# Encoder layer on one core: constant decay rows loaded early, first chunk's products first, merge panels split on ScalarE and VectorE

## The chip, the cores and the metric

One Trainium2 chip, one of its cores. The metric is device time of one execution in microseconds (us). TensorE (PE) multiplies, VectorE (DVE), ScalarE (ACT) and GpSimd (POOL) work elementwise, SyncE (SP) issues the transfers (DMA). Each engine takes its instructions in the order of its own list and waits at the first whose inputs or buffers are not ready. SBUF is the on-chip memory, PSUM the accumulators that TensorE writes.

## The reference

One layer over two groups of tokens, a prompt of 512 and a sample of 1024, so 1536 tokens of width 1024:

```python
h = rmsnorm(x, norm_pre_mix)
q, k, v, z, xbc, dt_raw, gates = split(h @ w_in)
att = rmsnorm(diff_attention(q, k, v, lam, rel_bias), subln_w)
xs, B, C = split(silu(conv(xbc)))
y = ssd_scan(xs, dt_f, A_f, B, C) + flip(ssd_scan(flip(xs), flip(dt_b), A_b, flip(B), flip(C))) + d_skip * xs
y_ssm = rmsnorm(y * silu(z), ssm_norm_w)
merged = sigmoid(g0) * (att @ w_proj_attn) + sigmoid(g1) * (y_ssm @ w_proj_ssm)
x = x + rmsnorm(merged @ w_out, norm_post_mix)
h = rmsnorm(x, norm_pre_ffn)
x = x + rmsnorm((silu(h @ gate) * (h @ up)) @ w_down, norm_post_ffn)
```

The scan of the state-space branch (SSD) works in 12 chunks of 128 tokens. Inside a chunk it needs exp(a_cum[i] - a_cum[j]) below the diagonal, "the decays", for each of 16 heads and both directions.

## The kernel before, in words

All products are in fp32, as three products each: every operand is split into a high and a low part (hi = rounded value, lo = value - hi), and hi*hi, hi*lo and lo*hi are summed in PSUM. Lines L165 to L167 are these three. A weight panel is 1024 rows by 256 columns. `split_panel` (L145) loads it in two halves of 128x4x256 into `wraw` (pool `rp`, two buffers) and splits each with `split` (L133) into `whi` and `wlo` (pool `wp`, two buffers each). `split` has four forms: the default `act_dve` casts on ACT (L136) and subtracts on DVE (L137); `act_pool` subtracts on GpSimd; with `pool`, GpSimd does both (L142 the cast, L143 the subtraction).

The stages follow one another: normalisation of the tokens in three pieces of 512 (here called chunks c, `hT`, feature-major, transposed on TensorE, L203 to L205); projections for v, q, k, gates, dt and XBC, with attention over heads alongside; the SSD part with the projection for z alongside; the merge of both branches and the output projection; the feed-forward part. Intermediate tensors go through DRAM (`v_d`, `z_d`, `xs_d`, `ac_d`, `g_d` and so on). The order of each engine's list is set by a scheduler which simulates the program on its own timeline; the source only gives the data flow and the buffers.

**Start.** For c = 0, 1, 2: four token tiles are loaded, squared (ACT), scaled (L395, DVE) and transposed. After all three, the first two panels of v are loaded and split with `pool`, and their products are made per chunk.

**Decays.** One product with a matrix of 119 rows gives the decays. Its right operand `segr` (two tiles of 119 x 2048, one a direction) has 24 rows that depend on the steps (from `ac_d`, hi and lo, 12 each) and 95 constant rows (`c_neg`); the left operand `sl`, per chunk, has 24 selecting rows, 32 rows from `ad_d` and 63 constant ones (`c_sel`). `segr` is filled in four pieces of 1024 columns: three loads into `raw` (one buffer), one cast on DVE (L652). `c_neg` is loaded at that point, behind the stores of `ac_d`. The backward scan follows on the same SP queue: it loads `xg` (L690) and `bg`, scales xg on GpSimd (`xw`, L673), makes the state product `st_ps` on TensorE (L675) and the product `yo_ps` (L697).

**dt.** `wd` (the dt panel, 128x8x64) goes through `wraw` too; its product is L531. The XBC panels follow.

**Merge and output projection.** Their order in the source is out_proj(0), merge(1), norms(0), out_proj(1), merge(2), norms(1), operands of the feed-forward part, out_proj(2), norms(2). `merge` (L896) has four panels of w_proj_attn; per half panel the gate (`gt`, ACT L903) and the other branch (`pt`) are loaded, and the product is evacuated by DVE L907 (reads PSUM), L908, ACT L909 and DVE L910 into the split tiles `big`. `out_proj` has four panels of w_out and is evacuated by ACT. `norms` runs L1063 and L1064 (DVE), L1071 (DVE) and transposes for the feed-forward part (L1075). All 20 panels of the three out_proj and the two merge calls here are split with `pool`.

## Time and profile before

| | before |
|---|---|
| median of 3 runs | 3239.67 us (3237.82 to 3248.19) |
| profiled execution | 3245.1 us |
| its span | 3243.3 us |
| TensorE busy | 3049.5 us (94%) |
| DVE, ACT, POOL busy | 57%, 37%, 32% |
| mean granted TensorE clock | 0.974 |

The span runs from the first to the last recorded instruction. "Busy" is the time in which an engine executes, not that it does so at full rate: the granted clock tells at which share of its full clock TensorE was let run. An idle stretch of TensorE is listed with the instruction that it waited for and whatever ended the wait ("<-").

### The profile page before, as it was taken

To read this page: it belongs to the slowest core of one execution; us is meant where nothing else is said; L and a number is where in the kernel's file an instruction comes from. 1 tells how busy PE (TensorE), PEld (TensorE's weight loads), DVE (VectorE), ACT (ScalarE), POOL (GpSimd) and SP (SyncE) were. 2 spreads that over 40 slices of the span, in tenths; PEclk is the share of its full clock that TensorE was granted. 3 is DMA by queue.
4 is the path that set the end of the run, shared out by engine and by line. 5 is a ranking of instruction groups with operands and counts; after the bars stand their busy time and mean duration, and the time that the engine had idled before them with its cause. 6 is when DMAs were issued, how large, how long until landed. Compare 5 with 4: busy or idle time off the path is not lost.

```text
span 3243.3 us, 44646 instructions
## 1 busy us (share of the span) xinstructions
PE 3049.5 (94%) x16667; PEld 2677.0 (83%) x16667; DVE 1842.6 (57%) x2913; ACT 1209.3 (37%) x2255; POOL 1034.0 (32%) x796
## 2 busy tenths in 40 slices
PE   7999999999899999899999888878999899989998
PEld 7988887888787778687887777778999899978787
DVE  5114443455228994487788664776656766632444
ACT  4003333333113433466666523243333333322343
POOL 1003332000143442377567344433333433210100
PEclk9999999999999999999999998888999899999999
DMA  4623332223554454755555055544333333363354
GB/s 146 194 96 116 112 99 83 69 72 110 165 174 132 149 157 147 205 173 164 162 148 159 30 191 182 187 140 135 99 99 97 101 96 101 105 202 100 117 165 131
DMA packets 443325, 430.36 MB, mean 133 GB/s; under 512 B 25356, under 2 KB 360417, under 8 KB 442045
## 3 DMA queue, kind: packets, MB, share of 16 engines
q1 hardware_dynamic: 443109, 427.52, 42.8%
q8 instruction: 131, 2.15, 0.3%
q14 instruction: 85, 0.70, 0.1%
HBM read 315.37 MB, written 120.44 MB: 134 GB/s over the span
## 4 chain that ended last, share of the span: by engine, by line
PE 63%; DMA 12%; DVE 10%; issue 6%; POOL 4%; ACT 3%; SPq 1%; POOLq 0%; ACTq 0%; DVEq 0%
PE acc L165 9%; PE acc L167 9%; PE acc L166 9%; PE mm L165 5%; PE mm L167 5%; PE mm L166 5%; PE d L167 4%; PE d L166 3%; PE d L165 3%; DMA araw<-r_d 1%; DMA raw<-k_d 1%; DMA wraw<-in_w_gate_up_dram 1%; DMA gt<-g_d 1%; PE yd L772 1%; PE st_ps L675 1%
## 5 line engine op out<-in xcount | busy, mean ns | idle before, releaser
L165 PE MATMUL acc<-hT,whi 128*128 128x512 f32 x1056 | 420.9, 399 | 2.8 <-ACT st L435 2.8
L166 PE MATMUL acc<-hT,whi 128*128 128x512 f32 x1056 | 416.1, 394 | 0.0
L167 PE MATMUL acc<-hT,wlo 128*128 128x512 f32 x672 | 263.7, 392 | 0.0
L297 ACT ACTIVATE pt<-pt,nm 128x1024 f32<-128x1024 f32 (+1 forms) x192 | 193.3, 1008 | 125.5 <-DVE nm L294 115.3
L165 PEld LDWEIGHTS acc<-hT,whi 128*128 128x128 f32 x1056 | 198.5, 188 | 47.9 <-issue 5.5
L294 DVE CUSTOM_DVE_ANT_0 pt<-s,tb 128x1024 f32<-128x1024 f32 (+1 forms) x192 | 197.6, 1040 | 64.4 <-PE s L292 51.2
L166 PEld LDWEIGHTS acc<-hT,whi 128*128 128x128 f32 x1056 | 198.6, 188 | 42.2 <-issue 3.6
L165 PE MATMUL acc<-whi,hT 128*128 128x256 f32 x768 | 226.3, 295 | 0.1
L166 PE MATMUL acc<-wlo,hT 128*128 128x256 f32 x768 | 225.2, 293 | 0.0
L167 PE MATMUL acc<-whi,hT 128*128 128x256 f32 x768 | 224.2, 292 | 0.0
L167 PE MATMUL d<-dhi,fl 128*128 128x512 f32 x528 | 207.8, 394 | 8.3 <-DVE fl L137 8.3
L165 PE MATMUL d<-dhi,fh 128*128 128x512 f32 x528 | 207.7, 393 | 8.3 <-ACT fh L136 8.3
L166 PE MATMUL d<-dlo,fh 128*128 128x512 f32 x528 | 207.1, 392 | 0.0
L137 DVE TENSOR_TENSOR fl<-raw,fh 128x896 fp32r<-128x896 f32 (+1 forms) x72 | 85.9, 1195 | 200.4 <-ACT fh L136 200.4
L165 PE MATMUL mm<-op,wy 128*128 128x384 f32 x528 | 178.8, 339 | 10.3 <-ACT op L136 8.1
L167 PE MATMUL mm<-op,wy 128*128 128x384 f32 x528 | 178.7, 338 | 0.7 <-DVE wy L137 0.7
L166 PE MATMUL mm<-op,wy 128*128 128x384 f32 x528 | 178.3, 338 | 0.0
L303 POOL TENSOR_SCALAR pt<-pt,zs 128x512 f32<-128x512 f32 (+1 forms) x96 | 88.2, 919 | 255.4 <-DVE zs L301 213.5
L232 POOL TENSOR_TENSOR ql<-raw,qh 128x512 fp32r<-128x512 f32 x48 | 63.2, 1331 | 299.6 <-ACT qh L229 295.5
L165 PEld LDWEIGHTS acc<-whi,hT 128*128 128x128 f32 x768 | 148.6, 194 | 9.9 <-issue 8.5
L136 ACT CAST fh<-raw 128x896 fp32r<-128x896 f32 (+1 forms) x72 | 70.8, 983 | 227.7 <-PE d L166 212.7
L167 PE MATMUL acc<-hT,whi 128*128 128x512 f32 x384 | 155.5, 405 | 0.0
(358 smaller groups left out, 8612.6 us busy)
## 6 DMA issues: line engine op xcount, KB each, us to landing
wraw<-in_w_in_dram SPq DMA_DIRECT2D x60, 512.0 KB
wraw<-in_w_gate_up_dram SPq DMA_DIRECT2D x92, 256.0 KB
raw<-ff_d SPq DMA_DIRECT2D x48, 448.0 KB
wr<-in_w_gate_up_dram SPq DMA_DIRECT2D x80, 256.0 KB
ff_d<-c SPq DMA_DIRECT2D x88, 192.0 KB
g_d<-st SPq DMA_DIRECT2D x48, 256.0 KB
xg<-xs_d SPq DMA_DIRECT2D x48, 256.0 KB
gt<-g_d SPq DMA_DIRECT2D x48, 256.0 KB
```

Source lines behind the costliest of these rows:

```text
L136: S.copy(hi, raw)
L137: V.tensor_sub(lo, raw, f(hi))
L165: TE.matmul(ps, ah, bh, start=(i == 0), stop=False)
L166: TE.matmul(ps, ah, bl, start=False, stop=False)
L167: TE.matmul(ps, al, bh, start=False, stop=(i == n - 1))
L232: G.tensor_sub(q_l[:, s_], q_r[:, s_], f(q_h[:, s_]))
L294: V.tensor_tensor_reduce(out=pt[:], in0=sps[:], in1=tb[:, off:off + SL], scale=-1.0, scalar=3.0e38, op0=ALU.add, op1=ALU.min, accum_out=nm ...
L297: S.activation(out=pt, in_=pt, func=AF.Exp, bias=nm[:, m:m + 1], scale=-1.0, accum_out=(z0, zs[:, 0:1])[m])
L303: G.tensor_scalar(pm[1][:, cb], pm[1][:, cb], zs[:, 1:2], 0.0, op0=ALU.mult, op1=ALU.add)
L675: TE.matmul(ps, b_g, xw, start=True, stop=True)
L772: TE.matmul(yps[:, hs], ms[0][:, h, :], x_g[:, hs], start=True, stop=True)
```

## The change

- `segr` has 120 rows: 96 constant rows now come first, 24 step rows last, and `sl` accordingly (32 rows from `ad_d`, then 88 of `c_sel`: three loads instead of four). The constant rows are loaded in four loads of 96 x 1024 through `wraw` ahead of the dt panel, and cast on ACT. The step rows come late, in four loads of 12 x 2048 into two buffers of their own, and two ACT casts.
- v's first two panels are loaded directly behind chunk 0's tokens and split with a new form `pool_dve` (cast on GpSimd, subtraction on DVE). Chunk 0's products with the first panel follow chunk 0's transposes; those with the second panel come one chunk later.
- The panels of `merge` and `out_proj` are split with the default form, ACT and DVE.

```diff
-SEGK = 119
+SEGK = 120
...
     oh = (np.arange(32)[:, None] == bucket[None, :]).astype(np.float32)
     thr = np.arange(2, P, 2)
     sel = np.zeros((SEGK, 24, P), np.float32)
-    neg = np.zeros((2, SEGK - 24, NH, P), np.float32)
+    neg = np.zeros((2, 96, NH, P), np.float32)
     for r in range(24):
-        sel[r, [2 * (r % 12), 2 * (r % 12) + 1]] = 1.0
+        sel[96 + r, [2 * (r % 12), 2 * (r % 12) + 1]] = 1.0
     for r in range(32):
         neg[:, r, r % 16] = -1.0
-    sel[56:, 0::2] = (i[None, :] >= thr[:, None])[:, None, :]
-    sel[56:, 1::2] = (i[None, :] < thr[:, None])[:, None, :]
-    neg[0, 32:] = np.where(i[None, :] < thr[:, None], -1e30, 0.0)[:, None, :]
-    neg[1, 32:] = np.where(i[None, :] >= thr[:, None], -1e30, 0.0)[:, None, :]
-    return {"c_tri": c, "c_bucket": oh, "c_sel": sel, "c_neg": neg.reshape(2, SEGK - 24, NH * P)}
+    sel[32:95, 0::2] = (i[None, :] >= thr[:, None])[:, None, :]
+    sel[32:95, 1::2] = (i[None, :] < thr[:, None])[:, None, :]
+    neg[0, 32:95] = np.where(i[None, :] < thr[:, None], -1e30, 0.0)[:, None, :]
+    neg[1, 32:95] = np.where(i[None, :] >= thr[:, None], -1e30, 0.0)[:, None, :]
+    return {"c_tri": c, "c_bucket": oh, "c_sel": sel, "c_neg": neg.reshape(2, 96, NH * P)}
 
 
 @with_exitstack
...
     def split(hi, lo, raw, eng=None):
         if eng == "act_dve":
             S.copy(hi, raw)
+            V.tensor_sub(lo, raw, f(hi))
+        elif eng == "pool_dve":
+            G.tensor_scalar(hi, raw, 1.0, 0.0, op0=ALU.mult, op1=ALU.add)
             V.tensor_sub(lo, raw, f(hi))
         elif eng == "act_pool":
             S.copy(hi, raw)
...
         es = ExitStack()
         st0 = es.enter_context(tc.tile_pool(name="st0", bufs=4, reuse_waits="tile"))
         hT = []
+        def gemm_tm_pair(t, w):
+            ps = acc.tile([P, 2, 256], F32, tag="acc", name="acc")
+            for u in range(2):
+                gemm_tm(ps[:, u, :], w, hT[t // 4], slice((t + u) % 4 * P, ((t + u) % 4 + 1) * P))
+            return ps
+
+        def evac_v(p0, t, ps):
+            so = st0.tile([P, 2, 256], F32, tag="st0", name="st")
+            done = V.tensor_copy(so, ps)
+            store(out=v_d[t * P:(t + 2) * P, p0:p0 + 256].rearrange("(j p) n -> p j n", p=P), in_=so)
+            return done
+
         with tc.tile_pool(name="xa", bufs=2, reuse_waits="tile") as xa, tc.tile_pool(name="xa_ps", bufs=3, space=PSUM) as xps:
             natural_log_exp()
+            later = []
             for c in range(NCH):
                 dst = hp.tile([P, 2, KB, 512], F32R, tag="hT", name=f"hT{c}")
                 tiles = []
...
                     V.tensor_scalar(xt, xt, r[:, 0:1], 0.0, op0=ALU.mult, op1=ALU.add)
                 to_feature_major(xps, tiles, C_PRE, dst)
                 hT.append((dst[:, 0], dst[:, 1]))
+                for i in later:
+                    evac_v(i // 2 * 256, 4 * c - 4 + i % 2 * 2, gemm_tm_pair(4 * c - 4 + i % 2 * 2, first[i // 2]))
+                if c == 0:
+                    first = [split_panel(w_in[:, V0 + p0:V0 + p0 + 256], eng="pool_dve") for p0 in (0, 256)]
+                later = [2, 3]
+                for i in range(4 if c == NCH - 1 else 2):
+                    evac_v(i // 2 * 256, 4 * c + i % 2 * 2, gemm_tm_pair(4 * c + i % 2 * 2, first[i // 2]))
 
         def proj_fm(col0, ncol, evac, eng="act_dve", start=0):
             for p0 in range(start, ncol, 256):
...
                     so = st.tile([P, 512], F32, tag="st", name="st")
                     S.copy(so, ps)
                     store(out=g_d[r0:r0 + P, c * 512:(c + 1) * 512], in_=so)
-
-        def evac_v(p0, t, ps):
-            so = st0.tile([P, 2, 256], F32, tag="st0", name="st")
-            done = V.tensor_copy(so, ps)
-            store(out=v_d[t * P:(t + 2) * P, p0:p0 + 256].rearrange("(j p) n -> p j n", p=P), in_=so)
-            return done
-
-        first = [split_panel(w_in[:, V0 + p0:V0 + p0 + 256], eng="pool") for p0 in (0, 256)]
-        for c in range(NCH):
-            for i in range(4):
-                ps = acc.tile([P, 2, 256], F32, tag="acc", name="acc")
-                t = 4 * c + i % 2 * 2
-                for u in range(2):
-                    gemm_tm(ps[:, u, :], first[i // 2], hT[c], slice((t + u) % 4 * P, ((t + u) % 4 + 1) * P))
-                evac_v(i // 2 * 256, t, ps)
 
         with tc.tile_pool(name="pre2", bufs=1, reuse_waits="tile") as pre2, tc.tile_pool(name="pps2", bufs=2, space=PSUM) as pps2:
             lam = pre2.tile([P, 4, 64], F32, name="lam")
...
         dec = sp.tile([P, NT, 32], F32, name="dec")
         wst = sp.tile([P, NT, 32], F32, name="wst")
         segr = [sp.tile([SEGK, NH * P], F32R, name=f"segr{d_}") for d_ in range(2)]
+        for d_ in range(2):
+            for o in (0, 1024):
+                raw = staged(rp, [96, 1024], (None, a["c_neg"][d_][:, o:o + 1024]), tag="wraw")
+                S.copy(segr[d_][0:96, o:o + 1024], raw)
         dsk = sp.tile([P, NH], F32, name="dsk")
         load(out=dsk, in_=a["d_skip"].broadcast_to([P, NH]))
         wd = wp.tile([P, KB, 64], F32R, tag="whi", name="wd")
...
                 for i, t_ in enumerate((ah, al)):
                     store(out=d__[i].rearrange("(i c) h l -> (c h) i l", i=3), in_=f(t_[:, j]))
             for d_ in range(2):
-                for o in (0, 1024):
-                    os_ = slice(o, o + 1024)
-                    acv = [ac_d[s_].rearrange("(c d) h l -> c d (h l)", d=2)[:, d_, os_] for s_ in range(2)]
-                    raw = staged(dp, [SEGK, 1024], (slice(0, 12), acv[0]), (slice(12, 24), acv[1]),
-                                 (slice(24, SEGK), a["c_neg"][d_][:, os_]))
-                    V.tensor_copy(segr[d_][:, os_], raw)
+                acv = [ac_d[s_].rearrange("(c d) h l -> c d (h l)", d=2)[:, d_] for s_ in range(2)]
+                raw = staged(dp, [SEGK, NH * P], (slice(96, 108), acv[0]), (slice(108, 120), acv[1]), tag=f"raw{d_}")
+                S.copy(segr[d_][96:SEGK], raw[96:SEGK])
 
         dt_scope.close()
         sc = ph1.enter_context(tc.tile_pool(name="sc", bufs=2, reuse_waits="tile"))
...
             for c in range(lo_c, hi_c):
                 sl = sc.tile([SEGK, 2, P], F32R, tag="sl", name="sl")
                 acv = [ad_d[s_, 2 * c:2 * c + 2].rearrange("d h l -> h d l") for s_ in range(2)]
-                slr = staged(sc, [SEGK, 2, P], (slice(0, 24), a["c_sel"][0:24, 2 * c:2 * c + 2]),
-                             (slice(24, 40), acv[0]), (slice(40, 56), acv[1]),
-                             (slice(56, SEGK), a["c_sel"][56:SEGK, 2 * c:2 * c + 2]), tag="slr", bufs=1)
+                slr = staged(sc, [SEGK, 2, P], (slice(0, 16), acv[0]), (slice(16, 32), acv[1]),
+                             (slice(32, SEGK), a["c_sel"][32:SEGK, 2 * c:2 * c + 2]), tag="slr", bufs=1)
                 V.tensor_copy(sl, slr)
                 yz = wp.tile([P, 2, D], F32, tag="wlo", name="yz")
                 y, z = yz[:, 0], yz[:, 1]
...
             cs = slice(c * 512, (c + 1) * 512)
             hi, lo = big_pair()
             for p0 in range(0, D, 256):
-                w = split_panel(a["w_proj_attn"][0][:, p0:p0 + 256], eng="pool")
+                w = split_panel(a["w_proj_attn"][0][:, p0:p0 + 256])
                 for b in range(2):
                     r0 = p0 + b * P
                     kb = r0 // P
...
                 tiles = [mp.tile([P, D], F32, tag="mt", name="mt", bufs=4) for _ in range(4)]
                 sums = wk.tile([P, 4, 4], F32, tag="ms4", name="ms4")
                 for p0 in range(0, D, 256):
-                    w = split_panel(a["w_out"][0][:, p0:p0 + 256], eng="pool")
+                    w = split_panel(a["w_out"][0][:, p0:p0 + 256])
                     for j in range(4):
                         ps = mm_tile(256)
                         gemm_tm(ps, w, mT, slice(j * P, (j + 1) * P))
```

What the scheduler makes of it, at three places. The lists are those of one engine in order of issue; "x4" means four such instructions in a row.

SP at the start, up to chunk 1's tokens (`x_sample`); `wraw` is v's first panels. Before:

```order
L383 DMA prm<-in_subln_w_dram 1x128
L384 DMA prm<-in_conv_w_dram 60x128
L375 DMA xt<-in_x_sample_dram 128x1024 x4
L152 DMA wraw<-in_w_in_dram 128x4x256 x4
L375 DMA xt<-in_x_sample_dram 128x1024 x4
L152 DMA wraw<-in_w_in_dram 128x4x256 x2
```

With the change:

```order
L399 DMA prm<-in_subln_w_dram 1x128
L400 DMA prm<-in_conv_w_dram 60x128
L155 DMA wraw<-in_w_in_dram 128x4x256 x2
L391 DMA xt<-in_x_sample_dram 128x1024 x4
L155 DMA wraw<-in_w_in_dram 128x4x256 x4
L391 DMA xt<-in_x_sample_dram 128x1024 x4
```

The two halves of the first panel now go ahead of chunk 1's tokens, the second panel ahead of chunk 2's.

SP at the decays, behind the stores of `ac_d`, up to the first load of the backward scan (`xg`). Before:

```order
L131 DMA raw<-ac_d 12x1024 x4
L131 DMA raw<-in_c_neg_dram 95x1024
L645 DMA ad_d<-ah 128x3x128
L645 DMA ad_d<-al 128x3x128
L706 DMA z_d<-st 128x2x256
L131 DMA raw<-ac_d 12x1024 x2
L131 DMA raw<-in_c_neg_dram 95x1024
L706 DMA z_d<-st 128x2x256
L131 DMA raw<-ac_d 12x1024 x2
L131 DMA raw<-in_c_neg_dram 95x1024
L706 DMA z_d<-st 128x2x256
L690 DMA xg<-xs_d 128x512
```

With the change:

```order
L131 DMA raw_6447<-ac_d 12x2048
L131 DMA raw_6451<-ac_d 12x2048
L131 DMA raw_6447<-ac_d 12x2048
L131 DMA raw_6451<-ac_d 12x2048
L715 DMA z_d<-st 128x2x256
L657 DMA ad_d<-ah 128x3x128
L657 DMA ad_d<-al 128x3x128
L715 DMA z_d<-st 128x2x256
L699 DMA xg<-xs_d 128x512
L701 DMA bg<-bt_d 128x128
```

The loads of `c_neg` are gone from here, and with them the second and third round through `raw`; between the last load of step rows and `xg` two stores of `z_d` and two of `ad_d` are left.

DVE in merge(1), beside norms(0): `gt`, `big` and `araw` belong to the merge and the attention's third piece, `mt` to the norms, `wlo<-wraw,whi` is the subtraction of a panel's half. Before:

```order
L1064 TENSOR_TENSOR mt<-mt,xr 128x512
L907 SCALAR_TENSOR_TENSOR gt<-gt,mm 128x512
L908 TENSOR_TENSOR gt<-gt,pt 128x512
L1064 TENSOR_TENSOR mt<-mt,xr 128x512
L910 SCALAR_TENSOR_TENSOR big<-gt,big 128x512
L137 TENSOR_TENSOR big<-araw,big 128x512 x2
L1064 TENSOR_TENSOR mt<-mt,xr 128x512
L908 TENSOR_TENSOR gt<-gt,pt 128x512
L354 SCALAR_TENSOR_TENSOR araw<-araw,cols 128x512
L907 SCALAR_TENSOR_TENSOR gt<-gt,mm 128x512
L910 SCALAR_TENSOR_TENSOR big<-gt,big 128x512
```

With the change:

```order
L915 SCALAR_TENSOR_TENSOR gt<-gt,mm 128x512
L137 TENSOR_TENSOR wlo<-wraw,whi 128x1024 x2
L916 TENSOR_TENSOR gt<-gt,pt 128x512
L357 SCALAR_TENSOR_TENSOR araw<-araw,cols 128x512
L915 SCALAR_TENSOR_TENSOR gt<-gt,mm 128x512
L1072 TENSOR_TENSOR mt<-mt,xr 128x512 x2
L918 SCALAR_TENSOR_TENSOR big<-gt,big 128x512
L137 TENSOR_TENSOR big<-araw,big 128x512
L137 TENSOR_TENSOR wlo<-wraw,whi 128x1024
L916 TENSOR_TENSOR gt<-gt,pt 128x512
L137 TENSOR_TENSOR wlo<-wraw,whi 128x1024
```

Four subtractions of panel halves now stand among the merge's evacuations.

## Rows read from the trace of the kernel before

**Rows 1.** Page header: span; busy time, share and instructions of each engine.

```profile
span 3243.3 us, 44646 instructions
...
PE 3049.5 (94%) x16667; PEld 2677.0 (83%) x16667; DVE 1842.6 (57%) x2913; ACT 1209.3 (37%) x2255; POOL 1034.0 (32%) x796
```

**Rows 2.** Windows, start: us, busy by engine (instructions), granted clock, DMA share, GB/s.

```profile
10.00:30.00 20.00, 12.49 (x58) 10.10 (x58) 17.70 (x41) 11.79 (x30) 10.88 (x7) 0.91 0.64 212
```

**Rows 3.** Windows, decays.

```profile
840.00:860.00 20.00, 11.09 (x62) 8.83 (x61) 3.07 (x5) 0.60 (x1) 5.13 (x6) 0.74 0.53 151
```

**Rows 4.** Windows, merge and output projection.

```profile
1900.00:1950.00 50.00, 39.78 (x157) 31.21 (x156) 40.91 (x48) 12.40 (x29) 23.49 (x12) 0.90 0.64 214
1950.00:2000.00 50.00, 37.12 (x250) 34.93 (x249) 29.43 (x39) 17.56 (x44) 22.34 (x13) 0.83 0.66 213
2050.00:2100.00 50.00, 37.70 (x184) 30.67 (x183) 33.51 (x42) 16.00 (x31) 22.88 (x12) 0.83 0.69 231
2100.00:2200.00 100.00, 72.75 (x487) 70.12 (x486) 79.91 (x131) 42.61 (x117) 35.39 (x22) 0.89 0.43 135
```

**Rows 5.** Windows, the dt panel's stretch.

```profile
540.00:560.00 20.00, 13.51 (x83) 10.11 (x81) 7.10 (x22) 4.76 (x7) 1.60 (x5) 0.94 0.25 79
```

**Rows 6.** Timeline, start, POOL then DVE: start, duration, instruction.

```profile
19.62 2.41 POOL L143 TENSOR_TENSOR wlo<-wraw,whi 128x1024 fp32r<-128x1024 f32 x1
...
20.15 1.90 DVE L196 TENSOR_TENSOR rs<-rs,rs1t 128x1 f32<-128x1 f32 x1
```

**Rows 7.** Instructions of lines L137 and L136: ns least/median/most, first and last start, forms.

```profile
L137 DVE TENSOR_TENSOR wlo<-wraw,whi x40: 1208/1220/1951, 93.2 to 867.3; 128x1024 fp32r<-128x1024 f32 x40
...
L136 ACT CAST whi<-wraw x75: 617/1050/1065, 92.2 to 2175.7; 128x1024 fp32r<-128x1024 f32 x72, 128x512 fp32r<-128x512 f32 x3
```

**Rows 8.** TensorE's waits, 0 to 50 us: us in total, times, longest.

```profile
PE tr_ps L203 <- DVE hT L205: 5.4, 2, 2.7
```

**Rows 9.** Timeline, decays, SP's queue then DVE.

```profile
834.76 0.29 SPq L131 DMA_DIRECT2D raw<-in_c_neg_dram x1
...
843.62 0.47 SPq L690 DMA_DIRECT2D xg<-xs_d x1
...
841.33 0.69 DVE L652 CAST segr<-raw 119x1024 fp32r<-119x1024 f32 x1 [7.36 <-DMA raw<-in_c_neg_dram]
```

**Rows 10.** Chain that ended last, 815 to 900 us: start, us, what.

```profile
843.62 7.94 DMA xg<-xs_d
```

**Rows 11.** TensorE's waits, 800 to 900 us.

```profile
PE st_ps L675 <- POOL xw L673: 8.9, 1, 8.9
PE yo_ps L697 <- DVE yb L699: 2.6, 1, 2.6
```

**Rows 12.** Groups of POOL, 1850 to 2225 us: busy, mean ns | idle before.

```profile
L143 POOL TENSOR_TENSOR wlo<-wraw,whi 128x1024 fp32r<-128x1024 f32 x36 | 94.8, 2650 | 0.7
L142 POOL TENSOR_SCALAR whi<-wraw 128x1024 fp32r<-128x1024 f32 x36 | 41.3, 1153 | 160.8 <-PE mm L167 62.4 <-DMA wraw<-in_w_out_dram 49.8 <-DMA wraw<-in_w_proj_attn_dram 44.8
```

**Rows 13.** Groups of DVE, 1850 to 2225 us.

```profile
L1063 DVE SCALAR_TENSOR_TENSOR mt<-mt,mr,pmw 128x512 f32<-128x512 f32 x24 | 29.8, 1310 | 0.2
L1064 DVE TENSOR_TENSOR mt<-mt,xr 128x512 f32<-128x512 f32 x24 | 24.4, 1025 | 9.1 <-DMA xr<-in_x_sample_dram 9.1
L137 DVE TENSOR_TENSOR big<-araw,big 128x512 fp32r<-128x512 f32 x16 | 19.0, 1194 | 5.7 <-ACT big L136 5.5
...
L910 DVE SCALAR_TENSOR_TENSOR big<-gt,big 128x512 fp32r<-128x512 f32 x16 | 18.1, 1131 | 3.6 <-ACT big L909 3.5
...
L907 DVE SCALAR_TENSOR_TENSOR gt<-gt,mm 128x512 f32<-128x512 f32 x16 | 10.9, 679 | 5.1 <-ACT gt L903 5.1
```

**Rows 14.** TensorE's waits, 1850 to 2225 us.

```profile
PE tr_ps L1075 <- DVE mt L1071: 19.4, 7, 8.5
...
PE mm L167 <- POOL wlo L143: 13.1, 5, 6.6
...
PE mm L165 <- ACT big L909: 6.9, 3, 3.6
```

## Prediction

> **What bounds the kernel now.** I read the page's header first: TensorE is busy 94% of a 3243.3 us span [rows 1], so only the stretches where it idles or runs at a lower clock can pay. Then the table of windows, to find those stretches; then TensorE's waits in each, to see what released it; then the instructions of VectorE (DVE), GpSimd (POOL) and SyncE's queue there. Three places touch the change. At the start, 10 to 30 us, TensorE is busy 12.49 of 20 us [rows 2]. At the decays, 840 to 860 us, it is busy 11.09 of 20 at a granted clock of 0.74 [rows 3]. In the merge and output projections it loses (50 - 39.78) + (50 - 37.12) + (50 - 37.70) + (100 - 72.75) = 62.7 us between 1900 and 2200 us, 2000 to 2050 left aside, at granted clocks of 0.83 to 0.90 [rows 4]. A fourth place is where the new early loads land: 540 to 560 us, with 6.5 us idle already [rows 5].
>
> The profiled execution took 3245.1 us, 1.8 more than its span; the median of the three runs is 3239.67, 5.4 lower. I sum against 3245.1 and take the 5.4 off at the end. About 0.3%, 9.7 us, is what a measurement of this kernel can tell from no change.
>
> **A. Start.** Removed: four GpSimd subtractions, the first 2.41 us [rows 6], four stores of the order in which GpSimd alone splits the panels. Added: four DVE subtractions; the like of them on DVE takes 1.22 us in the middle [rows 7]. Moved: two panel loads on SP ahead of four token loads, and chunk 0's products ahead of chunk 1's normalisation. While GpSimd's subtraction ran from 19.62 to 22.03, a DVE operation on one column took 1.90 us [rows 6]: such stretching ends. On the path stand 5.4 us of TensorE waiting for DVE's feature-major evacuation [rows 8], and part of the idle time of [rows 2]. Against it: the new subtractions and squares of chunk 1, whose tokens now land later, stand ahead of some evacuations. Upper bound: all 7.5 us idle and the clock's 12.49 x 0.09 = 1.1, so 9; lower bound: nothing gained, and one panel's two subtractions, 2.4 us, late. I take -5, near the 5.4, since the products have work to put into exactly those gaps.
>
> **B. Decays.** Removed from SP and DVE at 820 to 850 us: four loads of 95 constant rows through one buffer and their four casts. One such load is issued at 834.76 and its cast runs at 841.33 [rows 9], 6.6 us; the next load must wait for that cast, and SP with it, so xg is issued only at 843.62 [rows 9] and lands 7.94 later [rows 10]. TensorE waits 8.9 us for it [rows 11]. Now four loads of 12 step rows go into two own buffers, and nothing stands between the last of them and xg but stores; xg is issued some 10 us earlier, about where the first of the removed waits began. TensorE's first state product also moves about 48 products forward; those stand behind it and fill the later gaps. Two new ACT casts of 24 rows by 2048 columns are off the path: DVE's 119 x 1024 took 0.69 us [rows 9], so twice the columns is some 1.4, and ACT is nearly idle there (0.60 of 20 us) [rows 3]. The products on the decays come later than the state products. Gain: 8.9 of waiting plus 11.09 x 0.26 = 2.9 of clock, less 1 for the first loads, so -11. Bounds: 0 if xg is late for another reason; -16 if the rest of the idle time goes too (8.9 idle + 2.9 + the 2.6 that the state product's other wait costs [rows 11], and some clock behind).
>
> **D. The price of B, at 540 to 560 us.** Four loads of 96 x 1024 go ahead through the two panel buffers, with four ACT casts; the like cast takes 1.05 us [rows 7], on an ACT busy 4.76 of 20 [rows 5]. SP meets a buffer that ACT must empty, so the small dt panel and the next panel come later. Two loads in a row through two buffers at the 6.6 us of [rows 9] would be 13 us if nothing covers them; TensorE has attention and projection work for 14 of these 20 us. Nearest is the small end, since two of the four are issued long before: +2; bounds -1 (the casts leave DVE) and +13.
>
> The row of [rows 9] shows 6.6 us for 380 KB. By the Trainium skill ("DMA: Bandwidth & Descriptors", section "Why a DMA increments its semaphore by 16 and not by 1") a transfer is spread over the largest count up to 16 that divides its rows: 95 rows give 5 engines, 96 rows 16. By that page each early load would be about 6.6 x 5/16 = 2.1 us, an estimate, and the upper bound of D would be +4 instead of +13; no run here shows it yet.
>
> **C. Merge and output projection.** Removed: 80 GpSimd instructions of 20 panels. Of these 72 lie in 1850 to 2225: 36 subtractions of 2650 ns and 36 casts of 1153 [rows 12]. Added there: 36 ACT casts of 1.05 us and 36 DVE subtractions of 1.22 us, 44 us [rows 7]. DVE pays less for them than that. Its operation that reads the products from PSUM takes 679 ns (L907), while four groups of the same tile that read SBUF twice take 1310, 1025, 1131 and 1194 [rows 13], and do so beside GpSimd's subtractions. Over their counts that is 15.1 + 8.3 + 7.2 + 8.2 = 39 us which I expect back. So DVE's total stays about level, 39 against 44, and small operations on columns return some more. What shortens is the latency of a panel: two casts and two subtractions were 2 x 1.15 + 2 x 2.65 = 7.6 us on one engine, now 2 x 1.05 + 1.22 = 3.3 with the two engines overlapping.
>
> Per term: of 13.1 us in which TensorE waits for GpSimd's low parts [rows 14] 9 go; the rest is the load itself. Of 19.4 + 6.9 us in which it waits for the normalised rows on DVE and for the merged tiles [rows 14], half goes, 13, since DVE's list is shorter just there. Clock: 39.78 x 0.10 + 37.12 x 0.17 + 37.70 x 0.17 + 72.75 x 0.11 = 24.7 us lost now [rows 4]; in proportion 22/62.7 of it, 9. Against: subtractions that now wait for TensorE to release a panel hold what is behind them on DVE, 3. Sum -28. Bounds: +5 (the new DVE work falls in its full stretches) and -50 (three quarters of idle time and clock loss go).
>
> **Sum.** -5 - 11 - 28 + 2 = -42; 3245.1 - 42 = 3203 for a run like the profiled one, 3198 from the median. I take **3200**.
>
> **Rivals.**
> *DVE becomes the bound of C.* For: it is busy 40.91 of 50 us at 1900 and 79.91 of 100 at 2100 [rows 4], and takes 44 us more. Against: the stretched 39 us. Then C gives only the waits for low parts, -9, with no clock: 3198 + 19 = about 3217. The Trainium skill ("Perfetto Trace Analysis", section "Optimizing Scalar/DVE Operations") says that with a saturated DVE moving work to ScalarE or even GpSimd may make sense, which speaks against this move; the DVE shares just named bear on that. 0.19.
>
> *Slower.* One mechanism: GpSimd sat idle 62.4 us before its casts waiting for TensorE to release a panel's buffers [rows 12]. These waits now stand in ACT's in-order queue, and ACT evacuates the projections and gates that TensorE's next products need. If all 62.4 reach TensorE, C is -28 + 62 = +34, and the whole +20: 3260. It decides from about 42 of the 62.4 on. Against: a second panel is ready by then, and ACT is busy only 42.61 of 100 us [rows 4]. 0.07.
>
> *C gives nearly all.* 62.7 + 24.7 less a quarter, some -62: 3164. It needs DVE to be the one cause of waiting; loads of panels keep GpSimd waiting too, 49.8 us [rows 12]. 0.10.
>
> *B and A do not do what they say* (xg waits for its stores, the start for its tokens): only C and D, -26: 3214. 0.12.
>
> **Numbers.** The forecast has 0.52. Range 3170 to 3232: up to the weak cases with A or B at nothing, down to C at its -50 with the rest; it leaves out the slower case and the far end of the third. Faster by over 9.7 us: the forecast, three rivals, less 0.05 where two weak ends meet, 0.88; within it 0.05; slower 0.07.
>
> **What would show it.** Right: the first st_ps before 841 us and no wait for xw; no GpSimd split in the merge, the merged-tile operations near 0.7 us; TensorE busy over 41 of 50 in the windows of [rows 4]; the XBC products within 3 us of where they began, relative to the work before. Wrong: ACT or DVE idle on TensorE ahead of evacuations, or new waits for the small dt panel over 5 us.

## The result and the profile after

| | before | with the change |
|---|---|---|
| median | 3242.39 us (4 runs, 3237.82 to 3248.19) | 3202.18 us (4 runs, 3200.6 to 3214.99) |
| ratio | | 0.9884, 95% interval 0.9853 to 0.9915 |
| profiled execution | 3245.1 us | 3200.6 us |
| its span | 3243.3 us | 3198.8 us |

40 us less, against 42 forecast and a predicted 3200. A second measurement of the same kernel gave 0.988 (0.986 to 0.9901). The sum came out right by luck: its terms were off in opposite directions, as the next sections show.

The page's header of the changed kernel answers to [rows 1]:

```profile
span 3198.8 us, 44610 instructions
...
PE 3040.4 (95%) x16667; PEld 2671.8 (84%) x16667; DVE 1814.7 (57%) x2953; ACT 1256.6 (39%) x2301; POOL 880.0 (28%) x712
```

DVE has 40 instructions more and is 28 us less busy: the first sign that what it did before was in part waiting inside its own instructions. POOL lost 154 us. The windows at the start, the decays, the dt panel and the merge answer to [rows 2 to 5] (us, busy time of PE, PEld, DVE, ACT and POOL with counts, granted clock, DMA share, GB/s):

```profile
10.00:30.00 20.00, 13.42 (x70) 11.26 (x71) 16.57 (x38) 11.61 (x30) 4.56 (x4) 1.00 0.69 235
840.00:860.00 20.00, 17.15 (x96) 13.16 (x95) 5.22 (x8) 0.60 (x1) 8.53 (x9) 0.91 0.57 175
540.00:560.00 20.00, 15.02 (x74) 10.55 (x72) 7.44 (x22) 7.62 (x12) 0.90 (x4) 0.83 0.61 177
1900.00:1950.00 50.00, 47.47 (x221) 39.17 (x219) 39.93 (x73) 25.55 (x43) 0.00 (x0) 0.97 0.82 286
1950.00:2000.00 50.00, 41.77 (x319) 40.15 (x318) 19.90 (x29) 25.15 (x61) 0.00 (x0) 0.93 0.51 161
2050.00:2100.00 50.00, 49.19 (x410) 48.81 (x409) 29.10 (x46) 30.93 (x79) 0.00 (x0) 1.00 0.56 178
2100.00:2200.00 100.00, 70.35 (x357) 65.18 (x356) 77.53 (x134) 41.37 (x84) 38.35 (x24) 0.81 0.47 150
```

TensorE is busier at the start by 0.9 us, at the decays by 6.1, and in the three windows shown between 1900 and 2100 by 7.7, 4.7 and 11.5. The last window holds the next stage already, in which TensorE still idles for 30 us.

For a ledger I matched TensorE's instructions of two traces by name and number and took the median shift of their starts, in us against the trace of before (one profiled execution against one). A negative entry is time gained in that stretch (stretches by the clock of before; not shown: 2200 to 2400 us, and 2600 to the end, which is within 1.3 of nothing in all but one run):

| profile | start, to 400 | dt, 400-600 | decays, 600-1000 | scan, 1000-1250 | attention, 1250-1850 | merge, 1850-2200 | 2400-2600 |
|---|---|---|---|---|---|---|---|
| forecast | -5 | +2 | -11 | 0 | 0 | -28 | 0 |
| the change | -1.3 | +0.9 | -6.4 | +2.7 | +7.7 | -40.5 | -6.3 |
| the change, again | -2.7 | -0.4 | -8.1 | +2.5 | +5.3 | -37.3 | -9.3 |

### The profile page after: what moved, and what is told of

Its sections match the earlier page's. It is cut to its first block, busy times and chain, and to the rows that moved or that the text cites. A ratio compares the mean times of both kernels' runs of the same rounds, so it can differ in the third digit from the quotient of the medians.

```text
span 3198.8 us, 44610 instructions
## 1 busy us (share of the span) xinstructions
PE 3040.4 (95%) x16667; PEld 2671.8 (84%) x16667; DVE 1814.7 (57%) x2953; ACT 1256.6 (39%) x2301; POOL 880.0 (28%) x712
## 5 line engine op out<-in xcount | busy, mean ns | idle before, releaser
L169 PEld LDWEIGHTS acc<-hT,whi 128*128 128x128 f32 x1056 | 199.6, 189 | 42.5 <-issue 3.6
L137 DVE TENSOR_TENSOR fl<-raw,fh 128x896 fp32r<-128x896 f32 (+1 forms) x72 | 86.0, 1195 | 200.1 <-ACT fh L136 200.1
L136 ACT CAST whi<-wraw 128x1024 fp32r<-128x1024 f32 (+1 forms) x115 | 116.0, 1037 | 201.1 <-PE acc L169 84.1
L137 DVE TENSOR_TENSOR wlo<-wraw,whi 128x1024 fp32r<-128x1024 f32 x80 | 95.4, 1222 | 114.2 <-ACT whi L136 104.9
L136 ACT CAST fh<-raw 128x896 fp32r<-128x896 f32 (+1 forms) x72 | 70.7, 982 | 227.3 <-PE d L169 212.7
```

The costliest lines, as they stand in the source:

```text
L136: S.copy(hi, raw)
L137: V.tensor_sub(lo, raw, f(hi))
L169: TE.matmul(ps, ah, bl, start=False, stop=False)
```

## The experiments

They take the change apart first, and then ask why the merge gained.

**One part alone.** e_a has only the start's edits (`pool_dve`, first panels, `later`), e_b only the decays' (`SEGK`, `c_neg`, `raw0` and `raw1`, `slr`), e_c only these:

```diff
-                w = split_panel(a["w_proj_attn"][0][:, p0:p0 + 256], eng="pool")
+                w = split_panel(a["w_proj_attn"][0][:, p0:p0 + 256])
...
-                    w = split_panel(a["w_out"][0][:, p0:p0 + 256], eng="pool")
+                    w = split_panel(a["w_out"][0][:, p0:p0 + 256])
```

Expected of the start alone:

> Only the start is changed (first panel loaded ahead, split on GpSimd and DVE, products first). In the two traces the start moved TensorE's work by -1.3 us from 100 us on. Theory (the parts add up, and the start is worth what is seen behind it): -1 to -2 us at 200 us, and no measurable difference, 3236 to 3246. Rival (the start is worth the 5 us of the prediction and something behind hid it): -4 to -6 us at 200 us. The attention between 1260 and 1880 us, which came out 7.7 us slower with the whole change: theory of chance order says it stays within 3 us of before here; if it moves by over 5 us the start is its cause.

Of the decays alone:

> Only the decays are changed (constant rows early, step rows late). Theory (parts add): +0.5 to +1.5 us at 600 us from the early loads, -6 to -8 us from 820 to 960 us, st_ps first near 839 us instead of 852.8; 3230 to 3242 over all. Rival 1 (the constant rows' early loads are what costs): over +3 us at 600 us. Rival 2 (the slower attention of the whole change comes from this part): 1260 to 1880 us slower than before by over 5 us, and the whole at 3238 to 3246.

Of the panels alone:

> Only the panels of the merge and the output projection are split on ACT and DVE. Theory (nearly all of the gain is here): -38 to -43 us between 1880 and 2210 us, the whole at 3193 to 3206, the DVE operations on merged tiles near 0.69 us. Rival (the gain needs the other parts, or the prediction's -28 was right and chance added the rest): -25 to -32 us there, the whole at 3207 to 3216. If the attention is slower through the first two panels of the output projection, split on ACT and DVE at its end, 1720 to 1760 us shows +3 us here too.

Measured:

| profile | ratio, 95% | start | dt | decays | scan | attention | merge | 2400-2600 |
|---|---|---|---|---|---|---|---|---|
| e_a | 1.0008 (0.9993 to 1.0023) | -2.8 | +0.1 | +0.4 | +6.6 | -3.3 | -0.3 | -6.8 |
| e_b | 0.9975 (0.9963 to 0.9987) | 0.0 | +3.2 | -6.9 | +2.6 | -5.9 | -4.1 | -2.7 |
| e_c | 0.9881 (0.9859 to 0.9903) | +0.6 | +1.1 | -0.3 | +1.3 | -1.1 | -37.1 | -8.7 |

The panels alone are the whole gain that can be measured: 0.9881 against 0.9884. The decays are worth 8 us by themselves, the start nothing that can be measured (its -2.8 lies between its two theories). How far one profile can be trusted shows in the merge, which e_a and e_b don't edit: -0.3 and -4.1. In 2400 to 2600 us, where no edit of e_a, e_b or e_c reaches, all are 2.7 to 8.7 us ahead: so I take it that the profiled execution of before was a long one there, and that column as no part of the change. For the early loads, e_b shows +3.2, just past the 3 us of its rival; e_c, without any, shows +1.1.

**Start and decays together, and the change without the start.** The change showed the attention 7.7 us longer, where it edits nothing. e_ab leaves the panels as before, e_bc and bc5 (the same kernel, on two occasions) leave the start as before; change5 is the change itself.

> The change without the new start. The start alone made no difference to the whole (ratio 1.0008), the decays alone gave 0.9975, the panels alone 0.9881. Theory (parts add, small differences of order aside): 0.985 to 0.988, some 3188 to 3198 beside a kernel before of 3237. Rival (the gain of the decays is lost behind, whatever goes with it): 0.988 to 0.990, no better than the panels alone.

> The change itself once more, beside the version without the new start on one chip. In five profiles with both the start and the decays changed the attention (1260 to 1850 us) was 1.7 to 13.7 us longer than before, in four with not both 1.1 to 5.9 us shorter. Theory (the order that the scheduler writes for the attention is worse when both are changed): the attention again over 1 us longer, the whole at a ratio of 0.987 to 0.990. Rival (it varies from run to run): the attention may come out shorter, and the ratio equals that of the version without the new start.

> Decays and panels changed, start as before. Theory (order of the attention): ratio 0.984 to 0.987, under the change's by 0.002 or more, the attention shorter than before by 1 to 6 us. Rival: no difference to the change beyond its interval.

> Start and decays changed, panels as before. Theory (both together give the worse order of the attention): the attention 2 to 14 us longer than before, and the whole at 0.998 to 1.002, although both save 8 us before it. Rival (the panels' part is needed for it, through the two panels that are split at the attention's end): the attention shorter by 1 to 6 us, the whole at 0.995 to 0.997.

| profile | ratio, 95% | start | dt | decays | scan | attention | merge | 2400-2600 |
|---|---|---|---|---|---|---|---|---|
| e_bc | 0.986 (0.984 to 0.988) | +0.7 | +2.4 | -7.3 | +2.7 | -4.5 | -43.9 | -1.9 |
| bc5 | 0.9864 (0.9847 to 0.9881) | +1.0 | +2.7 | -5.3 | +0.4 | -3.9 | -43.2 | -2.7 |
| change5 | 0.988 (0.986 to 0.9901) | -2.7 | -0.4 | -8.1 | +2.5 | +5.3 | -37.3 | -9.3 |
| e_ab | 1.0012 (1.0001 to 1.0024) | -1.4 | -0.5 | -6.6 | +0.1 | +1.6 | -2.5 | -2.1 |

e_ab came out no faster than before although its profile is 8 us ahead until 1250 us (that profile is of the fastest of its 12 executions, 3232.91 us; their median is 3238.99), and e_b without the new start was 0.25% faster. In all seven profiles with both parts (the change's two, e_ab and four below) the attention was 1.6 to 13.8 us longer than in the trace of before; in the six with at most one of them it lay between 5.9 shorter and 0.1 longer. The two groups also differ there in the order of instructions, which the scheduler makes new for each kernel: of the change's 2919 TensorE instructions in the attention, 2756 to 2902 stand in the same sequence in the four runs below and 2869 in e_ab, 2098 to 2210 in before, e_a, e_b, e_c and e_bc. So beside the decays' edits the start gives its 2 us back, and more, somewhere else; that the order itself is the cause is argued from this coincidence and was not tried alone. The version without the new start has the lower ratio both times, but the intervals overlap and bc5 is 0.0016 under change5, not the 0.002 expected: it isn't shown to be faster than the change.

**Why the merge gained: GpSimd beside DVE, or the panel's long way through GpSimd.** e_two and e_long keep the change's panels on ACT and DVE and put GpSimd time back beside them, off the panel's way. Both add work whose output is not read; the rest is the change. e_two:

```diff
+        def beside(h):
+            nn = mp.tile([P, 128], F32, tag="nn", name="nn", bufs=1)
+            for j in range(8):
+                x = f(h)[:, j // 2, j % 2 * 128:j % 2 * 128 + 128]
+                G.tensor_sub(nn, x, x)
```

and e_long the same in two pieces of 512 columns (an 8-bit `nn`, so that it fits):

```diff
+            nn = mp.tile([P, 512], mybir.dt.float8e4, tag="nn", name="nn", bufs=1)
+            x = f(h).rearrange("p a c -> p (a c)")
+            for j in range(0, 1024, 512):
+                G.tensor_sub(nn, x[:, j:j + 512], x[:, j:j + 512], saturate=False)
```

`beside` is called behind each half's `split`. e_actpool and e_pooldve put one half of the split back on GpSimd (`eng="act_pool"`, `eng="pool_dve"` in the two calls).

> The whole change, and beside each half panel of the merge and the output projection GpSimd makes eight subtractions of 128x128 on the high part into a tile that nobody reads: the panel's way to TensorE stays as in the change, GpSimd is busy beside DVE again. Theory 1 (GpSimd's reading of SBUF holds up DVE's operations with two SBUF operands, and that was the loss): the merged-tile operations and the norms' operations go from 0.69 to 0.85 us and more, the whole to 3212 to 3235. Theory 2 (the loss was the panel's long way through GpSimd): they stay under 0.75 us, the whole within 6 us of the change, 3197 to 3208.

> The whole change, and beside each half panel of the merge and the output projection GpSimd makes two subtractions of 128x512 on the high part into a small tile that nobody reads (8-bit output, so that it fits): as much GpSimd time as the removed subtractions had (some 95 us), in longer pieces than the 0.63 us of the run with eight small ones, which gave back 7 of 40 us in the stage. Theory 1 (GpSimd's long reads hold up DVE): the merged-tile operations rise from 0.69 to 0.8 to 1.0 us, and 8 to 20 us of the 40 between 1880 and 2210 us are given back, the whole at 3208 to 3222. Theory 2 (the panel's long way through GpSimd was the loss): under 5 us are given back there, the whole at 3197 to 3207.

> The whole change, but the merge's and the output projection's panels are cast on ACT and subtracted on GpSimd: the long subtractions stay on the path and beside DVE, only the casts have left GpSimd. Both theories of the stage (reads held up; long way of a panel) expect that most of the gain is lost, 25 us or more of the 40, the whole at 3225 to 3242, DVE's merged-tile operations over 0.95 us. Third theory (the casts and the length of GpSimd's list were the trouble): over half of the gain stays, the whole at 3200 to 3222.

> The whole change, but those panels are cast on GpSimd and subtracted on DVE: the panel's way is as short as in the change (two casts of 1.05 us and one subtraction of 1.22 us behind them), GpSimd is busy some 38 us in one-operand casts. Theory 1 (GpSimd's reads hold up DVE): the merged-tile operations at 0.72 to 0.85 us, 3 to 10 us given back, the whole at 3203 to 3213. Theory 2 (way of a panel): within 4 us of the change in the stage, the operations under 0.72 us. If ACT's new casts had cost something, this is faster than the change in the stage.

| profile | ratio, 95% | GpSimd beside the merge | attention | merge |
|---|---|---|---|---|
| the change | 0.9884 (0.9853 to 0.9915) | none | +7.7 | -40.5 |
| e_pooldve | 0.9887 (0.9865 to 0.9908) | 36 casts, 42.5 us | +1.7 | -38.8 |
| e_two | 0.9918 (0.9894 to 0.9942) | 288 short subtractions, 181.6 us | +9.6 | -33.8 |
| e_actpool | 0.9922 (0.9901 to 0.9942) | 36 long subtractions, 91.9 us, on the path | +2.8 | -20.4 |
| e_long | 0.9991 (0.9976 to 1.0006) | 72 subtractions, 106.5 us, off the path | +13.8 | -10.6 |

e_long shows that GpSimd beside DVE is enough to lose most of it. The panel's way has the same instructions as in the change, ACT's 36 casts waited 6.6 us for loads and never for GpSimd to release a buffer, and 30 of the 40 us of the stage are gone again. That is more than the 8 to 20 that I expected, and more than any stretch without an edit moved (13.8); with the longer attention the whole gain is gone. e_two came out between its theories: 7 us given back, the merged-tile operations at 0.80 us. One ACT cast there waited 2.5 us until GpSimd had read the buffer, so its 7 us are not DVE's alone. Groups of DVE, first in the change and then in e_long (line, operation, shapes and count | busy us, mean ns | idle before), 1850 to 2190 and 1850 to 2215 us:

```profile
L137 DVE TENSOR_TENSOR wlo<-wraw,whi 128x1024 fp32r<-128x1024 f32 x36 | 43.1, 1221 | 32.6 <-ACT whi L136 32.6
L1071 DVE SCALAR_TENSOR_TENSOR mt<-mt,mr,pmw 128x512 f32<-128x512 f32 x24 | 18.2, 834 | 0.1
...
L916 DVE TENSOR_TENSOR gt<-gt,pt 128x512 f32<-128x512 f32 x16 | 11.0, 690 | 9.5 <-DMA pt<-part_d 9.4
...
L918 DVE SCALAR_TENSOR_TENSOR big<-gt,big 128x512 fp32r<-128x512 f32 x16 | 11.0, 688 | 2.7 <-ACT big L917 2.6
L915 DVE SCALAR_TENSOR_TENSOR gt<-gt,mm 128x512 f32<-128x512 f32 x16 | 11.0, 685 | 2.5 <-ACT gt L911 1.8 <-PE mm L170 0.5
```

```profile
L137 DVE TENSOR_TENSOR wlo<-wraw,whi 128x1024 fp32r<-128x1024 f32 x36 | 59.0, 1662 | 33.1 <-ACT whi L136 33.1
L1079 DVE SCALAR_TENSOR_TENSOR mt<-mt,mr,pmw 128x512 f32<-128x512 f32 x24 | 23.0, 1027 | 0.1
...
L926 DVE SCALAR_TENSOR_TENSOR big<-gt,big 128x512 fp32r<-128x512 f32 x16 | 14.7, 920 | 2.8 <-ACT big L925 2.7
L924 DVE TENSOR_TENSOR gt<-gt,pt 128x512 f32<-128x512 f32 x16 | 14.3, 893 | 2.5 <-DMA pt<-part_d 2.5
...
L923 DVE SCALAR_TENSOR_TENSOR gt<-gt,mm 128x512 f32<-128x512 f32 x16 | 10.8, 677 | 1.0 <-ACT gt L919 1.0
```

The operations with two SBUF operands (L916, L918, the panel's subtraction) are long only beside GpSimd. Taken one by one: in the change, none of L916's sixteen meets a GpSimd instruction, and they take 683 to 694 ns; in e_long the twelve that meet none take 675 to 693 and the other four 1522 to 1530; before, ten take 677 to 692 and six, beside GpSimd, up to 2827. The one that takes an operand from PSUM (L907 before, L915, L923) has 679, 685 and 677 ns in the three traces, and 672 to 690 in e_two, where all sixteen run beside GpSimd. The GpSimd group of e_long:

```profile
L891 POOL TENSOR_TENSOR nn<-whi 128x512 fp8e4<-128x512 f32 x72 | 106.5, 1479 | 173.4 <-ACT whi L136 169.2
```

The Trainium skill ("SBUF — State Buffer", section "Who interferes with whom") states just this: a DVE instruction with two SBUF inputs contends with a GpSimd instruction that reads SBUF. The traces agree, with 893 against 690 ns. Whichever starts second waits for the whole instruction of the other, as the page also has it, and one place of e_long shows it in both directions, DVE then POOL:

```profile
1942.74 1.23 DVE L137 TENSOR_TENSOR wlo<-wraw,whi 128x1024 fp32r<-128x1024 f32 x1 [1.73 <-ACT whi L136]
1943.88 1.53 DVE L924 TENSOR_TENSOR gt<-gt,pt 128x512 f32<-128x512 f32 x1
1945.33 2.06 DVE L137 TENSOR_TENSOR wlo<-wraw,whi 128x1024 fp32r<-128x1024 f32 x1
```

```profile
1942.85 2.02 POOL L891 TENSOR_TENSOR nn<-whi 128x512 fp8e4<-128x512 f32 x1 [11.78 <-ACT whi L136]
```

DVE's first subtraction started ahead of GpSimd's and takes its usual 1.23 us; GpSimd's takes 2.02, where its shortest takes 1.03. The next operation of DVE starts inside GpSimd's, which ends at 1944.87, and ends only at 1945.41. That also fits that 288 pieces of 631 ns cost 7 us and 72 of 1479 ns cost 30, while the GpSimd time is the larger in the former.

e_pooldve and e_actpool tell which part of the split had to leave GpSimd. Of the panels' split in the merge, e_pooldve has, against before, only the subtractions moved and gains 38.8 us; e_actpool has only the casts moved and gains 20.4. That is half, where both theories of that run expected most of the gain to be lost; so the third theory holds in part: the casts were a burden too as long as the subtractions were on the same engine. With the subtractions gone, GpSimd's casts cost next to nothing, although the two long groups L916 and L1071 rose beside them from 690 to 859 and from 834 to 963 ns, above the 0.72 to 0.85 us expected: a longer DVE operation need not cost TensorE anything. ACT's 36 new casts cost nothing either, since on GpSimd instead they gain nothing. What stays open is how the loss before divides between DVE held up and the panel's long way: in e_long DVE has the panels' subtractions as well, which it had not before.

TensorE's waits of the change, 1850 to 2190 us (us in total, times, longest), against [rows 14]:

```profile
PE mm L168 <- ACT whi L136: 16.5, 2, 14.2
PE tr_ps L1083 <- DVE mt L1079: 6.8, 1, 6.8
PE mm L170 <- DVE wlo L137: 4.0, 3, 2.5
...
PE mm L168 <- ACT big L917: 1.9, 2, 1.4
```

and of e_long, 1850 to 2215 us:

```profile
PE mm L170 <- ACT whi L136: 19.2, 2, 17.1
PE mm L170 <- ACT big L925: 11.0, 3, 4.7
PE tr_ps L1091 <- DVE mt L1087: 10.5, 2, 7.7
PE mm L172 <- DVE wlo L137: 8.8, 3, 4.3
```

The merged tiles, the norms and the low parts are late again, all three through DVE. The first line in both is of the feed-forward part that follows.

**The same elsewhere.** If that is so, it should pay wherever TensorE waits for DVE. e_bcx is e_bc with GpSimd's last two long splits of the late stages moved:

```diff
-            ops.build(("b22",), V, "act_pool")
+            ops.build(("b22",), V, "act_dve")
...
-                    split(hi[:], lo[:], raw[:, k:k + 2], "pool" if (k0 + k) % 6 == 4 else "act_dve")
+                    split(hi[:], lo[:], raw[:, k:k + 2], "act_dve")
```

> As the version without the new start, with two more splits off GpSimd: every third pair of the down projection's weight rows and one group of the feed-forward operands. If GpSimd's long subtractions hold up DVE wherever both work, a further 2 to 8 us, 3183 to 3190. If they matter only where TensorE waits for DVE, as in the merge, no difference: TensorE waits for DVE's low parts 8.7 us in all in the down projection, and most of the rest of that stage is busy.

3180.23 us, ratio 0.9826 (0.9812 to 0.984), whose interval lies below the others' on that chip: the version to keep. It is 10.9 us under bc5, more than the 2 to 8 expected. The gain is at the change of weights in the middle of the down projection. The window of bc5, then that of e_bcx:

```profile
2980.00:3030.00 50.00, 45.24 (x190) 36.87 (x189) 29.69 (x24) 20.18 (x25) 14.62 (x6) 0.93 0.44 135
```

```profile
2980.00:3030.00 50.00, 50.00 (x222) 41.42 (x221) 29.47 (x37) 26.91 (x35) 0.00 (x0) 1.00 0.50 151
```

In bc5 the subtractions of the weights on DVE beside GpSimd's take 1583 ns in the mean, in e_bcx 1217:

```profile
L137 DVE TENSOR_TENSOR dlo<-draw,dhi 128x1024 fp32r<-128x1024 f32 x16 | 24.6, 1583 | 1.4 <-ACT dhi L136 1.4
```

```profile
L137 DVE TENSOR_TENSOR dlo<-draw,dhi 128x1024 fp32r<-128x1024 f32 x21 | 24.4, 1217 | 1.2 <-ACT dhi L136 1.2
```

Twenty-one take no more of DVE's time than sixteen did. In the ledger e_bcx is -8.5 us between 2600 us and the end, where the others are -1.3 at most. Its two edits were not run apart, so what each is worth is not shown.

## Why the prediction was right, point by point

**The bound and the places.** The three places were where the time was. The total held because two terms that were too large stood against one that was too small, with stretches that I hadn't on the list; that they cancel within 2 us was luck.

**A, start: -5, measured -1.3 and -2.7, and -2.8 alone.** The idle time at the start fell by less than I took. What I priced too low stood in the same term, "the new subtractions and squares of chunk 1, whose tokens now land later, stand ahead of some evacuations"; what the longest wait shows is a subtraction ahead of the scaling of chunk 0's last token tile. DVE's timeline of the change, then TensorE's:

```profile
16.59 1.23 DVE L140 TENSOR_TENSOR wlo<-wraw,whi 128x1024 fp32r<-128x1024 f32 x1 [1.00 <-POOL whi L139]
17.73 0.75 DVE L411 TENSOR_SCALAR xt<-xt,rs 128x1024 f32<-128x1024 f32 x1
```

```profile
18.54 0.90 PE L206 MATMUL tr_ps<-ident,xt 128*128 128x128 f32 x3 [3.26 <-DVE rs0v L194]
19.94 0.55 PE L168 MATMUL acc<-whi,hT 128*128 128x256 f32 x1 [0.50 <-ACT hT L207]
```

The 5.4 us of waiting for DVE [rows 8] became one of 3.26 us. The trace names `rs0v`, the last DVE instruction before it, but what is transposed at 18.54 is the tile scaled at 17.73, and that scaling waited behind a subtraction that itself waited 1.00 us for GpSimd's cast. Products run from 19.94. The whole-kernel forecast for this part, a gain, didn't come: 1.0008.

**B, decays: -11, measured -6.4 and -8.1, -6.9 alone.** The mechanism is as forecast. SP issues xg at 834.42 instead of 843.62 [rows 9], the first state product runs at 839.06 instead of 852.8, and the wait of 8.9 us is 0.9. SP's timeline, then TensorE's:

```profile
834.42 0.43 SPq L699 DMA_DIRECT2D xg<-xs_d  x1
```

```profile
839.06 1.13 PE L684 MATMUL st_ps<-xw,bg 128*128 128x512 f32 x2 [0.94 <-POOL xw L682]
```

Mis-sized was the gain of "8.9 of waiting" less 1, with products that "fill the later gaps": the scan has waits of its own, which move up with it. TensorE's waits between 800 and 1000 us are now:

```profile
PE yo_ps L706 <- DVE yb L708: 2.7, 1, 2.7
PE st_ps L684 <- issue: 2.7, 2, 1.8
PE st_ps L684 <- POOL xw L682: 0.9, 1, 0.9
PE yd L780 <- DVE m L777: 0.7, 1, 0.7
```

These are 7.0 us, against 8.9 + 2.6 = 11.5 before [rows 11]: 4.5 gained where the term had 7.9. The wait for `yb` stays as it was; the 2.7 of `st_ps` and the 0.7 of `yd` are new. The clock's 2.9 came in size (3.0, from a granted clock of 0.91 instead of 0.74 between 840 and 860 us and 1.00 instead of 0.91 between 880 and 900). The starts of the scan moved by 13.7 us, TensorE's work by 7.

**D, early loads: +2, measured +0.9 and -0.4, +3.2 alone.** In size right. The loads of 96 rows are quick: two are issued at 539.55, and ACT casts them at 543.49 and 544.92:

```profile
543.49 1.04 ACT L526 CAST segr<-wraw 96x1024 fp32r<-96x1024 f32 x1 [2.05 <-DMA wraw<-in_c_neg_dram]
544.92 1.04 ACT L526 CAST segr<-wraw 96x1024 fp32r<-96x1024 f32 x1
```

That is 768 KB in 5.4 us from the first issue to the second cast, where 380 KB of 95 rows took 6.6 [rows 9]. The rule in the Trainium skill ("DMA: Bandwidth & Descriptors", section "Why a DMA increments its semaphore by 16 and not by 1"), by which 96 rows spread over 16 engines and 95 over 5, agrees with that in direction; the count of engines itself is in no row here, and the first of the two loads took 3.9 us to its cast, not the 2.1 of the estimate. The upper bound of 13 us was never near.

**C, merge: -28, measured -37 to -44 in the five profiles above that have it.** The mechanism was right: of the 39 us that I expected back from four groups of DVE, 34 came back (834, 711, 688 and 688 ns instead of 1310, 1025, 1131 and 1194 [rows 13]; of the 24 that make the 834, the 21 that meet no GpSimd instruction take 745 to 755). DVE's total fell rather than staying level (231 to 201 us between the same products, 1850 to 2200 us before and 1853.6 to 2163.1 in the change), since groups that I had left out shrank too: L908, now L916, from 1117 to 690 ns, L354, now L357, from 1186 to 750. Mis-sized were three terms. "Half goes": of 19.4 us for the norms [rows 14] 6.8 are left and of 6.9 for the merged tiles 1.9, so 17.6 went instead of 13; the low parts, 13.1 to 4.0, gave the 9 of the forecast. Idle time and clock: between the same products TensorE's idle time in all fell from 65.8 to 37.9 us and what the lower clock costs from 24 to 12, so 28 and 12 where the forecast had 22 and 9. And the 3 against it did not come: DVE's panel subtractions waited for ACT's casts alone. The latency of a panel, which I named as what shortens, was not enough: e_long has it short, but for DVE's stretched subtraction, and loses three quarters.

**The rivals.** DVE didn't become the bound: 39.93 + 19.90 = 59.8 us busy from 1900 to 2000 us in the change, 70.3 before [rows 4], although the panels' subtractions have come to it. The rule of the Trainium skill weighed there ("Perfetto Trace Analysis", section "Optimizing Scalar/DVE Operations"), that a saturated DVE may gain from work moved to GpSimd, is not borne out in this stage: taking work from GpSimd relieved DVE. The prediction gave that passage by half; it goes on that the two share an SBUF read port, so that moving work between them might not help, and with that the traces agree. Nor did the waits for released buffers reach ACT's list: before its panel casts it idled 10.5 us, 7.4 of it for loads and 3.1 for TensorE, of the 62.4 us that the slower case needed. "C nearly all", -62, wasn't reached; -40.5 lies nearer to the -28 of the forecast. The far bound of C, -50, is not the "three quarters" that the prediction calls it: three quarters of 62.7 + 24.7 are 66, the value of that rival. Of "B and A do not do what they say", A's half held: the start gained the whole kernel nothing.

**Not on the list.** +2.7 in the scan, +7.7 in the attention, -6.3 at 2400 to 2600. The last I take as before's own variation. The other two, 10.4 us, cost more than the start and the decays brought.

## What to carry to other kernels

Where GpSimd and DVE both work on SBUF, don't read a long mean on DVE as its work: compare it with an operation of the same shape that takes an operand from PSUM, or with its own least duration, and count the difference as what GpSimd costs DVE; TensorE pays only where it waits for DVE. Take long two-operand work off GpSimd first in such places; short pieces hurt less than long ones of the same total. And where a scheduler writes the order anew, price a part by the shift of the products behind it, not by the wait that it removes: waits of the same chain move up, and far stretches change by as much.

## What I had not expected of the hardware

The same wait can cost the clock or not. Between 1205 and 1210 us before, and 1198 and 1203 after, TensorE idles 1.5 us on the same products. Before, then after:

```profile
1205.00:1210.00 5.00, 3.48 (x19) 2.45 (x18) 4.75 (x7) 1.16 (x4) 2.15 (x2) 1.00 0.77 238
1210.00:1215.00 5.00, 4.97 (x25) 3.81 (x25) 5.00 (x10) 2.85 (x7) 0.00 (x0) 1.00 0.70 198
```

```profile
1198.00:1203.00 5.00, 3.48 (x18) 2.48 (x17) 4.75 (x7) 1.20 (x4) 2.12 (x2) 0.97 0.82 240
1203.00:1208.00 5.00, 5.00 (x15) 3.70 (x16) 4.40 (x9) 2.40 (x7) 0.00 (x0) 0.50 0.66 188
1208.00:1213.00 5.00, 5.00 (x20) 4.02 (x19) 4.04 (x6) 1.63 (x4) 2.58 (x2) 0.84 0.50 156
```

Before, the granted clock stayed at 1.00; after, it fell to 0.50 (1.2 GHz) behind the gap and came back within 10 us. In these windows the lower clock costs 5.00 x 0.50 + 5.00 x 0.16 = 3.3 us, about the +2.7 of the scan's column in this profile, with no wait to show for them. What decided it stays open.
